# High and low values side by side as 128 weight columns: two products instead of three in the attention of a dilated gMLP decoder

## The chip, the core and the metric

The kernel runs on one NeuronCore of a Trainium2 chip. The time is the device time of one execution in microseconds; the median of three runs is compared. TensorE multiplies (PE in the profile, its weight loads are PEld), VectorE (DVE), ScalarE (ACT) and GpSimd (POOL) do the elementwise work, and SyncE (SP) starts the transfers.

## What is computed

One step of a decoder with two layers. Each layer projects 1024 prompt positions and 64 sample positions (8 streams of 8), mixes them in two branches, a gated gMLP and an attention, and adds the result to the residual stream. The part that matters here is the attention of the prompt: three groups with dilations 1, 4 and 16, eight heads of 64 dimensions each, in which a query reads its own and at most 128 earlier keys of its residue class.

```python
def dilated_band_attention(q, k, v, dil, n_back):
    ...
    s = jnp.einsum('brnqhd,brnkhd->brnhqk', qb, kb,
                   preferred_element_type=jnp.float32) * (HEAD_DIM ** -0.5)
    ...
    s = jnp.where(valid[None, None, :, None], s, NEG)
    lse = jax.nn.logsumexp(s, axis=-1)
    p = jnp.exp(s - lse[..., None])
    o = jnp.einsum('brnhqk,brnkhd->brnqhd', p.astype(vb.dtype), vb,
                   preferred_element_type=jnp.float32)
    ...
    return o, lse

def combine_dilations(outs, lses):
    w = jax.nn.softmax(jnp.stack(lses, axis=0), axis=0)
    return jnp.sum(w[..., None] * jnp.stack(outs, axis=0), axis=0)
```

Everything is fp32.

## The kernel before

**Precision.** The big products run in fp32r, which keeps fewer bits than fp32. Each operand is therefore split into a high part (a rounded copy, by ScalarE) and a low part (the rest, by a subtraction), and a product becomes three: high by high, high by low, low by high. `split` (L242 to L249) makes the parts.

**The stream of jobs.** A layer goes through a list of jobs, each of which multiplies a 128-column slice of the projection weights with the activations of three pieces of 384, 384 and 320 positions (`piece`, L733). A piece is 24 products into a bank `pspj` (L741), three for each of eight key tiles. Between them, behind the 9th, the 18th and the last product, `tick` (L445) lets other work into the instruction streams. Every engine executes its own stream in the order in which it was written, so what stands ahead and waits holds back what stands behind.

**Attention.** A unit is one group and one pair of heads: jobs for values, queries and keys of 128 columns (two heads), 24 units in all, 12 in each layer. A unit has eight blocks of 128 queries, and each block passes three steps, one piece apart. `att_a`: TensorE multiplies queries and keys into `pss` (L870), VectorE adds the mask and takes the extremes (L878), ScalarE takes the exponential (L882). `att_b`: TensorE transposes the probabilities into `pspt` (L895), and ScalarE and VectorE split them into the high and low tile `pt` (every other block uses a spare part of an activation tile, named `act` in the profile). `att_c`, which the change touches: the products of values and probabilities into `pso` (L916), and one ScalarE copy for each head out of `pso` into `oacc` (recorded at L240, in `copy`). A block has one key block or two: always one in the group with dilation 16, alternating in the group with dilation 4, and two but for the first block with dilation 1.

**Values.** `ev_val` (L817) takes a value job out of PSUM. `v_transposes` (L832) transposes four blocks of 128 positions at a time on TensorE (L838) into a `psmi` bank, and `split` writes a tile `vhl` of [128, 2, 512]: 512 high columns, then 512 low ones. A head of a key block is 64 columns in each half.

**Merging.** When the three groups of a head pair are done, `combine` (L958) computes the softmax weights of the groups on a small tile: a chain of eight VectorE operations with one of ScalarE between them (L969 to L977) and a split `ehl`; later it multiplies and adds the three `oacc` tiles (L993 to L999). There are four merges in each layer.

**Buffers.** `pspj` has three banks, `pss` two, and `pspt`, `pso` and `psmi` one each. The next `att_c` can therefore start only when `pso` has been read.

Of the kernel before, what the change touches and what calls it, by code (L numbers as in the profile page):

```python
# [25 lines left out]
FR = mybir.dt.float32r  # L26
AF = mybir.ActivationFunctionType
OP = mybir.AluOpType
# [151 lines left out]
class Builder:  # L180
# [636 lines left out]
    def ev_val(self, l, job, p, ps, st):  # L817
        _, g, pr = job
        if p == 0:
            st["t"] = self.slot([128, T], name="vT")  # L820
        for o, x in self.group_views(st["t"], ps, g, p):
            self.copy(o, x)
        if p == 2:
            t = st["t"]
            self.store(self.a["ov"][l, g, pr], t)
            u = {"l": l, "g": g, "pr": pr, "n": 3 * pr + 2 - g}
            self.cur = u
            u["v"] = [self.slot([128, 2, 512], FR, "vhl") for _ in range(2)]
            for i in range(3):
                self.after(lambda i=i: self.v_transposes(u, t, i), i + 1)  # L830

    def v_transposes(self, u, t, i):  # L832
        nc, ident = self.nc, self.pk("ident")
        if i < 2:
            ps = self.ps("mi")
            for j in range(4):
                b = 4 * i + j
                nc.tensor.transpose(ps[:, j * 128:j * 128 + 128], t[:, b * 128:b * 128 + 128], ident)  # L838
            self.split(u["v"][i][:, 0, :], u["v"][i][:, 1, :], ps)
        else:  # L840
            self.rows_out(t[:, SEQ:T], self.vn_d[u["l"]][u["g"], :, u["pr"] * 128:u["pr"] * 128 + 128])

# [59 lines left out]
    def att_c(self, u, b):  # L902
        nc, g = self.nc, u["g"]
        n = 1 + self.nprev(g, b)
        pt = u["pt"].pop(b)
        ps = self.ps("o")
        for h in range(2):
            first = True
            for j in range(n):
                kb = b - n + 1 + j  # L910
                v = u["v"][kb // 4]
                c = slice((kb % 4) * 128 + 64 * h, (kb % 4) * 128 + 64 * h + 64)
                i = slice(128 * (h * n + j), 128 * (h * n + j) + 128)
                for a, e in ((0, 0), (0, 1), (1, 0)):
                    last = j == n - 1 and a == 1
                    nc.tensor.matmul(ps[0:64, 128 * h:128 * h + 128], v[:, a, c], pt[:, e, i], start=first, stop=last)  # L916
                    first = False
        o = self.oacc[:, u["n"] % 6, :]
        for h in range(2):
            r = slice(64 * h, 64 * h + 64)  # L920
            src = ps[0:64, 128 * h:128 * h + 128]
            if g == 2:
                dst = o[r, 128 * b:128 * b + 128]
            elif g == 1:
                dst = o[r].rearrange("p (m r b i) -> p r b m i", m=4, r=4, b=2, i=32)[:, b // 2, b % 2]
                src = src.rearrange("p (m i) -> p m i", i=32)
            else:
                dst = o[r].rearrange("p (r b i) -> p b r i", r=16, b=8, i=8)[:, b]
                src = src.rearrange("p (r i) -> p r i", i=8)
            self.copy(dst, src)  # L930
        if b == 7:
            for x in ("q", "k", "v"):
                del u[x]
            self.side.append(self.unit_stats(u))
# [770 lines left out]
```

## Time and profile before

| | |
|---|---|
| median of three runs | 3126.67 us (3125.6 to 3132.71) |
| the profiled execution | 3128.81 us |
| its span | 3127.0 us |
| TensorE busy | 3001.5 us, 96%, 19136 products |
| VectorE busy | 1702.8 us, 54% |
| ScalarE busy | 1230.0 us, 39% |
| GpSimd busy | 1363.7 us, 44% |
| mean granted clock of TensorE | 0.983 |

The profile shows one execution. Its page gives the busy time of each engine, the chain of work that ended last, and the costliest groups of instructions; the trace answers questions on a line, a tile or a stretch of time. Durations of products overlap, since TensorE starts the next one before the last has left the array, so what a product costs in a stream is the distance from its start to the next start. In a timeline, instructions of one kind that follow each other stand in one row with their count; the length of that row runs from the first start to the last end.

### The profile page before, as it was taken

The page shows a single profiled execution, that of the slowest core. Times are in us where ns is not written, and L with a number is a line of the kernel's source. Part 1 is how long each engine was busy: PE and PEld are TensorE (multiplying, and loading weights), DVE is VectorE, ACT ScalarE, POOL GpSimd, SP SyncE. Part 2 cuts the span into 40 slices and gives each one's busy share as a digit, 9 for nine tenths or more (in the row PEclk, how much of TensorE's full clock was granted, in tenths as well). Part 3 has the DMA queues.
Part 4 walks back from the last instruction along what each step waited for, and adds up shares of the span by engine and source line. Part 5 has one row for each costly group of instructions (what it writes and reads, how often), then busy time and mean ns, then how long its engine had stood idle before and what let it go on. Part 6 is the DMA issues. An engine that isn't in the chain of part 4 may idle for free.

```text
span 3127.0 us, 51203 instructions
## 1 busy us (share of the span) xinstructions
PE 3001.5 (96%) x19136; PEld 2860.7 (91%) x19136; DVE 1702.8 (54%) x3583; ACT 1230.0 (39%) x3085; POOL 1363.7 (44%) x959
## 2 busy tenths in 40 slices
PE   6998999999999999999999989999999999999998
PEld 4998899989999998879989988999999899999998
DVE  7444545463266656466773555464632757553666
ACT  5454444444233133343434544444442331322433
POOL 4665547463144223123446655564731542322343
PEclk8999999999999999999999999999999999999999
DMA  6335243434354334466544253434344542434665
GB/s 223 117 100 113 97 88 119 94 107 95 111 189 142 105 119 163 162 239 228 194 161 130 91 121 99 88 123 85 119 88 128 176 150 89 137 103 144 220 214 178
DMA packets 251537, 425.93 MB, mean 136 GB/s; under 512 B 103852, under 2 KB 158392, under 8 KB 251288
## 3 DMA queue, kind: packets, MB, share of 16 engines
q1 hardware_dynamic: 251288, 422.65, 44.7%
q8 instruction: 151, 2.47, 0.3%
q14 instruction: 98, 0.80, 0.1%
HBM read 349.96 MB, written 72.61 MB: 135 GB/s over the span
## 4 chain that ended last, share of the span: by engine, by line
PE 82%; DVE 7%; DMA 4%; issue 2%; ACT 2%; POOL 1%; SPq 0%; DVEq 0%; ACTq 0%; POOLq 0%
PE pspj L741 53%; PE pspj L1377 13%; PE pss L870 4%; PE pso L916 3%; PE pspt L895 2%; DMA kq<-in_kc_dram 1%; DMA craw<-in_wada_dram 1%; PE psmi L602 1%; DVE chl L249 1%; PE psmi L993 1%; PE pspt L1310 1%; DVE act L249 1%; PE pspt L1127 1%; PE pso L1127 1%; PE pss L1094 1%
## 5 line engine op out<-in xcount | busy, mean ns | idle before, releaser
L741 PE MATMUL pspj<-act,whi 128*128 128x384 f32 (+1 forms) x7680 | 1965.8, 339 | 6.2 <-DVE act L674 3.7
L741 PEld LDWEIGHTS pspj<-act,whi 128*128 128x128 f32 x7680 | 1350.9, 190 | 42.1 <-issue 6.6
L741 PE MATMUL pspj<-act,wlo 128*128 128x384 f32 (+1 forms) x3840 | 1263.0, 329 | 2.3 <-POOL wlo L247 2.3
L249 POOL TENSOR_TENSOR wlo<-wraw,whi 128x1024 fp32r<-128x1024 f32 x154 | 373.2, 2424 | 906.0 <-ACT whi L243 764.4
L741 PEld LDWEIGHTS pspj<-act,wlo 128*128 128x128 f32 x3840 | 728.2, 190 | 3.4 <-POOL wlo L247 3.4
L1377 PE MATMUL pspj<-act,whi 128*128 128x384 f32 (+1 forms) x1536 | 373.5, 326 | 0.5 <-ACT act L243 0.4
L243 ACT ACTIVATE whi<-wraw 128x1024 fp32r<-128x1024 f32 x280 | 294.0, 1052 | 124.3 <-DMA wraw<-in_wgm_dram 49.4
L247 POOL TENSOR_TENSOR wlo<-wraw,whi 128x512 fp32r<-128x512 f32 x126 | 192.2, 1532 | 325.5 <-ACT whi L243 274.7
L882 ACT ACTIVATE ssb<-ssb,ast 128x128 f32<-128x128 f32 (+1 forms) x384 | 170.2, 444 | 380.4 <-DVE ast L878 380.4
L878 DVE CUSTOM_DVE_ANT_0 ssb<-pss,pack 128x128 f32<-128x128 f32 (+1 forms) x384 | 119.4, 348 | 326.7 <-PE pss L870 325.7
L1377 PEld LDWEIGHTS pspj<-act,whi 128*128 128x128 f32 x1536 | 270.2, 188 | 1.0 <-ACT act L243 0.7
L1377 PE MATMUL pspj<-act,wlo 128*128 128x384 f32 (+1 forms) x768 | 250.3, 326 | 0.3 <-POOL wlo L247 0.3
L1005 ACT ACTIVATE th<-pspj 128x384 f32<-128x384 f32 x168 | 79.2, 471 | 422.3 <-PE pspj L741 375.9
L787 POOL TENSOR_TENSOR r<-r,sin 128x384 f32<-128x384 f32 x144 | 139.1, 966 | 175.7 <-DVE r L786 169.9
L249 DVE TENSOR_TENSOR chl<-craw,chl 128x512 fp32r<-128x512 f32 x182 | 155.4, 882 | 86.8 <-ACT chl L243 85.1
L377 POOL TENSOR_TENSOR kq<-kq,qb 128x1024 f32<-128x1024 f32 x64 | 152.6, 2390 | 66.5 <-DMA kq<-in_kc_dram 32.0
L381 POOL TENSOR_TENSOR kq<-kq,qb 128x512 f32<-128x512 f32 x128 | 167.3, 1312 | 30.3 <-DMA kq<-in_kc_dram 25.3
L386 DVE TENSOR_REDUCE sc<-kq 128x16 f32<-128x1024 f32 x128 | 155.7, 1217 | 13.0 <-POOL kq L377 12.9
L870 PE MATMUL pss<-kz,q 128*128 128x256 f32 x560 | 156.2, 387 | 5.6 <-ACT kz L240 5.6
L430 POOL TENSOR_TENSOR vq<-vq,pv 128x1024 f32<-128x1024 f32 x64 | 134.8, 2115 | 49.2 <-DMA vq<-in_vc_dram 25.9
L1377 PEld LDWEIGHTS pspj<-act,wlo 128*128 128x128 f32 x768 | 144.2, 188 | 0.6 <-POOL wlo L247 0.6
L247 DVE TENSOR_TENSOR wlo<-wraw,whi 128x512 fp32r<-128x512 f32 x126 | 108.0, 858 | 43.7 <-ACT whi L243 40.7
(211 smaller groups left out, 3676.6 us busy)
## 6 DMA issues: line engine op xcount, KB each, us to landing
wraw<-in_win_dram SPq DMA_DIRECT2D x160, 512.0 KB
kq<-in_kc_dram SPq DMA_DIRECT2D x64, 512.0 KB
vq<-in_vc_dram SPq DMA_DIRECT2D x64, 512.0 KB
craw<-in_wada_dram SPq DMA_DIRECT2D x48, 512.0 KB
wraw<-in_wgm_dram SPq DMA_DIRECT2D x48, 512.0 KB
wraw<-in_wo_dram SPq DMA_DIRECT2D x48, 512.0 KB
kq<-in_kc_dram SPq DMA_DIRECT2D x64, 256.0 KB
craw<-in_vc_dram SPq DMA_DIRECT2D x32, 512.0 KB
```

The costliest lines, as they stand in the source:

```text
L243: self.nc.scalar.activation(hi, src, AF.Copy)
L247: e.tensor_tensor(lo[:, c], src[:, c], hi[:, c].bitcast(FT), op=OP.subtract)
L249: (eng or self.nc.vector).tensor_tensor(lo, src, hi.bitcast(FT), op=OP.subtract)
L377: nc.gpsimd.tensor_tensor(v, v, x, op=OP.mult)
L381: nc.gpsimd.tensor_tensor(v[:, f], v[:, 1], x[f], op=OP.mult)
L386: nc.vector.tensor_reduce(sc[:, :, i].rearrange("p h j -> p j h"), ts.pop(i)[0].rearrange("p a (j h d) -> p (a j) h d", h=2, d=64), axis=A ...
L430: nc.gpsimd.tensor_tensor(v, v, p.unsqueeze(3).to_broadcast([128, 2, 8, 64]), op=OP.mult)
L741: nc.tensor.matmul(ps[:, :w], a[:, k, :], h[:, b, k, :w], start=(n == 0), stop=(n == 23))
L787: nc.gpsimd.tensor_tensor(t2, t2, self.sin[:, s], op=OP.mult)
L870: nc.tensor.matmul(s[:, 256 * j:256 * j + 256], u["q"][:, 128 * b:128 * b + 128], self.kz[:, (b - n + j) % 4].rearrange("p h c -> p (h c)" ...
L882: nc.scalar.activation(x[:, h, :w], x[:, h, :w], AF.Exp, bias=st[:, h * 8 + b:h * 8 + b + 1], scale=-1.0, accum_out=st[:, 16 + h * 8 + b:1 ...
L1377: self.nc.tensor.matmul(ps[:, :w], ws[a][:, k, :], hs[b][k][:, :w], start=(n == 0), stop=(n == 3 * nk - 1))
```

## The change

The tile of split values becomes [128, 4, 2, 128]: for each of four key blocks and each of two heads 128 columns, 64 high ones beside 64 low ones. For the first head the high values are the first 64 columns, for the second head the last 64. ScalarE and VectorE write them through access patterns with runs of 64 columns.

In `att_c` a product then has 128 weight columns, high and low, and there are two of them for a head and a key block, with the high and with the low probabilities. All 128 rows of `pso` are written: one half holds the sums of the high values, the other those of the low ones. The product of low values and low probabilities, left out before, is now in the sum.

On the way out, ScalarE copies the half with the low values to `oacc`, and a new VectorE instruction adds the half with the high values to it. Nothing else changes.

```diff
--- before.py
+++ after.py
@@ -825,7 +825,7 @@
             self.store(self.a["ov"][l, g, pr], t)
             u = {"l": l, "g": g, "pr": pr, "n": 3 * pr + 2 - g}
             self.cur = u
-            u["v"] = [self.slot([128, 2, 512], FR, "vhl") for _ in range(2)]
+            u["v"] = [self.slot([128, 4, 2, 128], FR, "vhl") for _ in range(2)]
             for i in range(3):
                 self.after(lambda i=i: self.v_transposes(u, t, i), i + 1)
 
@@ -836,7 +836,11 @@
             for j in range(4):
                 b = 4 * i + j
                 nc.tensor.transpose(ps[:, j * 128:j * 128 + 128], t[:, b * 128:b * 128 + 128], ident)
-            self.split(u["v"][i][:, 0, :], u["v"][i][:, 1, :], ps)
+            v = u["v"][i]
+            pst = list(v.ap[0])[0]
+            hi, lo = [bass.AP(tensor=v.tensor, offset=v.offset + o, ap=[[pst, 128], [256, 4], [w, 2], [1, 64]])
+                      for o, w in ((0, 192), (64, 64))]
+            self.split(hi, lo, ps.rearrange("p (b h d) -> p b h d", b=4, h=2))
         else:
             self.rows_out(t[:, SEQ:T], self.vn_d[u["l"]][u["g"], :, u["pr"] * 128:u["pr"] * 128 + 128])
 
@@ -908,17 +912,15 @@
             first = True
             for j in range(n):
                 kb = b - n + 1 + j
-                v = u["v"][kb // 4]
-                c = slice((kb % 4) * 128 + 64 * h, (kb % 4) * 128 + 64 * h + 64)
+                v = u["v"][kb // 4][:, kb % 4, h, :]
                 i = slice(128 * (h * n + j), 128 * (h * n + j) + 128)
-                for a, e in ((0, 0), (0, 1), (1, 0)):
-                    last = j == n - 1 and a == 1
-                    nc.tensor.matmul(ps[0:64, 128 * h:128 * h + 128], v[:, a, c], pt[:, e, i], start=first, stop=last)
+                for e in range(2):
+                    nc.tensor.matmul(ps[:, 128 * h:128 * h + 128], v, pt[:, e, i], start=first, stop=j == n - 1 and e == 1)
                     first = False
         o = self.oacc[:, u["n"] % 6, :]
         for h in range(2):
             r = slice(64 * h, 64 * h + 64)
-            src = ps[0:64, 128 * h:128 * h + 128]
+            src = ps[:, 128 * h:128 * h + 128]
             if g == 2:
                 dst = o[r, 128 * b:128 * b + 128]
             elif g == 1:
@@ -927,7 +929,8 @@
             else:
                 dst = o[r].rearrange("p (r b i) -> p b r i", r=16, b=8, i=8)[:, b]
                 src = src.rearrange("p (r i) -> p r i", i=8)
-            self.copy(dst, src)
+            self.copy(dst, src[64 - 64 * h:128 - 64 * h])
+            nc.vector.tensor_tensor(dst, dst, src[r], op=OP.add)
         if b == 7:
             for x in ("q", "k", "v"):
                 del u[x]
```

The order of the instructions, on TensorE, at the first block of all (`pso_1193` is its bank, `vhl_880` its values; L838 transposes values, L741 are products of the projection, and the line numbers behind the change are shifted); rows with - stand in the kernel before, with + in the changed one:

```order
 L741 MATMUL pspj_1142<-act_163,wlo_989 128x384
 L838 MATMUL psmi_1179<-pack,vT_1004 128x128 x4
-L916 MATMUL pso_1193<-pt_1108,vhl_880 64x128 x6
+L918 MATMUL pso_1193<-pt_1108,vhl_880 128x128 x4
 L741 MATMUL pspj_1202<-act_164,whi_988 128x320 x2
 L741 MATMUL pspj_1202<-act_164,wlo_989 128x320
```

Six products of 64 output rows have become four of 128; a block with two key blocks goes from twelve to eight. All else on TensorE stands where it stood.

On VectorE, at the end of the first merging, the kernel before (L977 and the split `ehl` are its last steps, L878 the masks of the next block, L249 the split of probabilities, L785 and L786 the rope of a job):

```order
L977 TENSOR_TENSOR ce_3033<-ce_3033,cmx_3032 16x384
L249 TENSOR_TENSOR ehl_3043<-ce_3033,ehl_3043 16x384
L878 ISA ssb_3067,ast_2579<-pss_3065,pack 128x128
L878 ISA ast_2579 128x1
L878 ISA ssb_3067,ast_2579<-pss_3065,pack 128x128
L878 ISA ast_2579 128x1
L249 TENSOR_TENSOR pt_3084<-pspt_3081,pt_3084 128x256
L785 TENSOR_TENSOR r_3101<-pspj_3055,cos_538 128x384
L786 STREAM_SHUFFLE r_3102<-pspj_3055 128x384
```

And the changed kernel at the same place, where L980, L882 and L933 are the merging, the masks and the new additions:

```order
L980 TENSOR_TENSOR ce_3011<-ce_3011,cmx_3010 16x384
L249 TENSOR_TENSOR ehl_3021<-ce_3011,ehl_3021 16x384
L933 TENSOR_TENSOR oacc_542<-oacc_542,pso_3024 64x128 x2
L882 ISA ssb_3045,ast_2565<-pss_3043,pack 128x128
L882 ISA ast_2565 128x1
L882 ISA ssb_3045,ast_2565<-pss_3043,pack 128x128
L882 ISA ast_2565 128x1
L249 TENSOR_TENSOR pt_3062<-pspt_3059,pt_3062 128x256
L785 TENSOR_TENSOR r_3079<-pspj_3033,cos_538 128x384
L786 STREAM_SHUFFLE r_3080<-pspj_3033 128x384
```

Two additions, one for each head, stand between the split `ehl` and the masks of the next block, and two more behind the rope instructions; so it is at each of the 192 blocks. ScalarE's and GpSimd's streams keep their instructions and their order.

## Rows read from the trace of the kernel before

**Rows 1.** The page: busy time of each engine; below, shares of the chain that ended last.

```profile
PE 3001.5 (96%) x19136; PEld 2860.7 (91%) x19136; DVE 1702.8 (54%) x3583; ACT 1230.0 (39%) x3085; POOL 1363.7 (44%) x959
...
PE 82%; DVE 7%; DMA 4%; issue 2%; ACT 2%; POOL 1%; SPq 0%; DVEq 0%; ACTq 0%; POOLq 0%
```

**Rows 2.** Busy us by engine (instructions) in the two attention stretches; then PEclk, DMA, GB/s.

```profile
100.00:700.00 600.00, 575.84 (x3842) 552.40 (x3840) 299.65 (x778) 271.00 (x833) 355.91 (x281) 0.98 0.41 107
1640.00:2330.00 690.00, 667.19 (x4495) 642.69 (x4494) 341.45 (x870) 313.33 (x947) 395.66 (x312) 0.98 0.41 105
```

**Rows 3.** Line 916: duration ns min/median/max, first and last start, form.

```profile
L916 PEld LDWEIGHTS pso<-act,vhl x960: 133/135/230, 129.5 to 2324.6; 128*64 128x64 f32 x192
L916 PE MATMUL pso<-act,vhl x960: 218/223/455, 129.5 to 2324.6; 128*64 128x128 f32 x192
...
L916 PE MATMUL pso<-pt,vhl x720: 218/223/304, 124.8 to 2320.3; 128*64 128x128 f32 x180
```

**Rows 4.** Timeline, PE: start us, length us, line, out<-in, count; a group of twelve.

```profile
602.05 0.88 PE L916 MATMUL pso<-act,vhl 128*64 128x128 f32 x12
602.77 0.56 PE L741 MATMUL pspj<-act,whi 128*128 128x384 f32 x2
```

**Rows 5.** Timeline, PE: a group of six and the stream behind it.

```profile
501.00 0.53 PE L916 MATMUL pso<-act,vhl 128*64 128x128 f32 x6
501.36 0.56 PE L741 MATMUL pspj<-act,whi 128*128 128x384 f32 x2
501.76 0.33 PE L741 MATMUL pspj<-act,wlo 128*128 128x384 f32 x1
501.94 0.51 PE L741 MATMUL pspj<-act,whi 128*128 128x384 f32 x2
502.28 0.33 PE L741 MATMUL pspj<-act,wlo 128*128 128x384 f32 x1
```

**Rows 6.** The page, costliest groups: busy us, mean ns of one, idle before.

```profile
L741 PEld LDWEIGHTS pspj<-act,whi 128*128 128x128 f32 x7680 | 1350.9, 190 | 42.1 <-issue 6.6
```

**Rows 7.** Timeline, PEld: the weight loads of line 579.

```profile
1356.04 0.96 PEld L579 LDWEIGHTS psmi<-pack,arow 18*128 18x128 f32 x8 [1.20 <-ACT arow L240]
```

**Rows 8.** Line 579: duration of one weight load.

```profile
L579 PEld LDWEIGHTS psmi<-pack,arow x96: 181/187/333, 20.0 to 1363.5; 18*128 18x128 f32 x96
```

**Rows 9.** Timeline, PE: four transposes.

```profile
510.81 0.60 PE L895 MATMUL pspt<-pack,ssb 128*128 128x128 f32 x4
```

**Rows 10.** Groups by shape: busy us, mean ns of one, idle before.

```profile
L895 PE MATMUL pspt<-pack,ssb 128*128 128x128 f32 x560 | 94.5, 276 | 21.3 <-DVE act L249 21.3
...
L878 DVE CUSTOM_DVE_ANT_0 ssb<-pss,pack 128x128 f32<-128x128 f32 x208 | 51.8, 286 | 175.9 <-PE pss L870 175.1
```

**Rows 11.** What writes or reads tile pso: duration ns min/median/max.

```profile
L240 ACT ACTIVATE oacc<-pso x384: 249/269/273, 125.6 to 2325.2; 64x128 f32<-64x128 f32 x192
...
L1130 DVE SCALAR_TENSOR_TENSOR sp<-pso,ng,bs x64: 339/343/345, 1062.0 to 2661.6; 128x128 f32<-128x128 f32 x64
...
L1327 DVE TENSOR_TENSOR zbs<-pso,zbs x16: 175/182/183, 917.5 to 2780.2; 64x32 f32<-64x32 f32 x16
```

**Rows 12.** Timeline, all engines, at the end of a merging.

```profile
298.53 0.53 ACT L240 ACTIVATE oacc<-pso 64x128 f32<-64x128 f32 x2
...
298.65 0.55 DVE L249 TENSOR_TENSOR ehl<-ce,ehl 16x384 fp32r<-16x384 f32 x1 [0.67 <-ACT ehl L243]
...
299.11 0.90 PE L916 MATMUL pso<-act,vhl 128*64 128x128 f32 x6 [4.41 <-ACT oacc L240]
299.13 0.27 DVE L878 CUSTOM_DVE_ANT_0 ssb<-pss,pack 128x128 f32<-128x128 f32 x1
```

**Rows 13.** Waits of PE from 100 to 700 us: total us, times, longest.

```profile
PE pspt L895 <- DVE act L249: 11.1, 3, 5.1
PE pso L916 <- ACT oacc L240: 4.4, 1, 4.4
```

## Prediction

> **What bounds the kernel now.** I read the busy table and the chain of waits first [rows 1]: TensorE is busy for 96% of the span and 82% of the chain that ended last lies on it, VectorE has 7% of that chain. Then I asked for the busy times of the two stretches, one in each layer, in which the prompt's attention runs [rows 2]: TensorE 575.84 of 600 us and 667.19 of 690 us, VectorE half busy (299.65 of 600, 341.45 of 690). So in the stage that the change touches TensorE issues nearly without a break, and what counts is how long its instruction stream is. It stands still for 24.2 us in the first stretch and 22.8 us in the second (length less busy time); the largest waits of the first stretch are few and long [rows 13]: the transposes of the probabilities (L895) wait for VectorE's split L249 three times for 11.1 us together, and L916 waits once for 4.4 us for ScalarE's copy out of `pso`.
>
> The next view is line 916 itself, the products that the change rewrites [rows 3]: 960 + 720 = 1680 products, each with its own weight load of 64 columns, although two neighbours use the same weights. 1680 is 104 blocks with one key block (6 products each) and 88 with two (12 each): 24 units of 8 blocks, of which the order of the keys gives 13 and 11 in every three units.
>
> **What a product costs in the stream.** The recorded duration of a product (223 ns) overlaps that of the next, so the price is the distance between starts. In a group of twelve [rows 4] the first starts at 602.05 and the next projection product at 602.77: 0.72 us, 60 ns each. In a group of six [rows 5]: 501.00 to 501.36, again 60 ns. A moving operand of 128 columns and a weight load of 64 columns both fit into 60 ns, and this row alone does not say which of them sets it.
>
> Other rows do. Line 579 multiplies 128-column weights with a moving operand of only 10 columns. Eight of its weight loads in a row span 0.96 us [rows 7], and one lasts 0.187 us [rows 8], so they start (0.96 - 0.187)/7 = 110 ns apart. Ten moving columns can't need that; the load of 128 weight columns does. Four transposes with 128-column loads and 128 moving columns span 0.60 us [rows 9], one 0.276 us [rows 10]: (0.60 - 0.276)/3 = 108 ns. These are plain fp32. That fp32r weights cost the same is seen at the end of each group of L916: the projection product that follows has 128 fp32r weight columns, and its load can hide only behind one short product. In [rows 5] the two products after the group then take 501.76 - 501.36 = 0.40 us, where two of them take 502.28 - 501.94 = 0.34 us in the steady stream behind. So that load needed 60 + 55 or so = 115 ns. The recorded durations agree: 190 ns for the projection's 128-column load [rows 6], 135 ns for the 64-column load [rows 3], 55 ns more.
>
> **The change part by part.**
> *Products.* Each head and key block goes from three products to two, so 560 of 1680 fall away and 1120 stay. Each now loads 128 columns, since high and low values lie side by side. With a load of 112 ns (the middle of 108 to 115) that the product before it can't cover, a block with one key block costs 4 x 112 = 448 ns, the last of these being the seam to the projection, against 6 x 60 + 55 = 415 ns: 33 ns more. A block with two costs 8 x 112 = 896 against 12 x 60 + 55 = 775 ns: 121 ns more. Sum: 104 x 0.033 + 88 x 0.121 = 3.4 + 10.6 = **14 us longer**. With 108 ns it is 104 x 0.017 + 88 x 0.089 = 9.6 us, with 115 ns 4.7 + 12.8 = 17.5 us. Nothing hides it: TensorE has no gaps between those groups [rows 2]. The saving in multiplications is real, but the array waits for weights, and there are 1120 x 128 columns to load now, where 1680 x 64 were loaded.
>
> [...]
>
> *Copy and add.* ScalarE's copy out of `pso` stays: 384 of 64x128 at 269 ns [rows 11]. New are 384 additions on VectorE, one behind each copy, reading `pso` and `oacc`. No row has this form. The bounds are 0.18 us (L1327, 64x32 out of PSUM) and 0.34 us (L1130, 128x128 out of PSUM) [rows 11]; I take 0.29, of L878, which reads 128 columns of PSUM beside SBUF [rows 10]. That is 384 x 0.29 = 111 us of VectorE's time, some 55 us in each attention stretch, which lifts it from 50% to 59% there. The cover is VectorE's idle half. An addition stands behind the two rope instructions of its piece (L785, L786) or behind other work, and waits for ScalarE's copy; queued behind it are the next block's masks (L878), the cache scores (L386) and the split of the probabilities (L249). TensorE asks for `pso` again one piece later, so an addition that ends half a microsecond after the copy delays nobody there.
>
> The cover is gone where VectorE is the late engine: at the merging of the three groups (L969 to L977 and the split behind them), three times in each attention stretch. In [rows 12] the split of the combining weights runs to 299.20; ScalarE's two copies are done at 299.06, and at 299.11 the waiting products of L916 start. With the change, two additions stand behind that split in VectorE's queue: 299.20 + 2 x 0.29 = 299.78 before `pso` is free, and the masks that started at 299.13 start there as well: 0.65 us later. One such pair at each of six places is 4 us; none would be 0, two pairs would be 8. I take **4 us**.
>
> *Layout.* The 48 splits of the values write in runs of 64 columns instead of 512; the same number of elements and instructions, so 0, with TensorE's transposes of other blocks as cover; if strided writes cost ScalarE or VectorE a tenth, it is a few us off the path.
>
> **Sum.** The profiled execution took 3128.81 us (span 3127.0). 3128.8 + 14 + 4 = 3146.8 us. The median of the runs shown is 3126.67, 2.1 us less than that execution; for a median I predict **3145 us**, 0.6% more. Its own range runs from 9.6 + 0 to 17.5 + 8: 3136 to 3152.
>
> **The rivals.**
> *B, the wide load is no dearer (faster).* If the load of 128 fp32r columns ran at the pace of 64, each product would stay at 60 ns: 1120 x 60 = 67.2 us instead of 100.8, 33.6 us less, and with the 4 us of VectorE the median would be 3126.7 - 33.6 + 4 = 3097. For it speaks only that no row has an fp32r load of 128 columns directly before a product of 128 moving columns. It decides from a distance of 90 ns downward (1120 x 90 = 100.8). [...] Chance 7%.
>
> *C, no change.* The load is partly covered, at some 86 ns: 1120 x 86 = 96.3, 4.5 us gained, which the 4 us of VectorE take back: 3126 us. [...] Against it: every row with 128 columns. Or the low end of the main case with a lucky turn at the stalls (9.6 us longer, some of it falling into TensorE's waits): 3133. Chance 14%.
>
> *D, VectorE becomes late (much slower).* The added instructions wait for ScalarE in VectorE's queue. If in one block of ten the pair of additions and the pair of copies before it (2 x 0.29 + 2 x 0.27 = 1.1 us) end up on the path, 192 x 0.1 x 1.1 = 21 us come on top of the 14: 3126.7 + 35 = 3162. For it: TensorE's long waits in this stage already are waits for VectorE [rows 13], `pso` and `pspt` have one buffer each, and after each merging VectorE has to catch up with less spare time. Against it: half of VectorE's time is free. Chance 17%.
>
> **How the numbers follow.** Main case 62%, B 7%, C 14%, D 17%. The predicted time is the main case, 3145. A measurement can tell about 0.3%, 9.4 us, from no change: slower is over 3136, faster under 3117. So slower 0.79, same 0.14, faster 0.07. The range leaves out B, the lower end of C and the upper part of D: 3126 to 3165.
>
> **What would show it.** In the changed kernel's trace the groups of four products should start 110 ns apart, a group of eight taking about 0.9 us to the next steady projection product; the recorded weight load should be near 190 ns. The additions should appear 384 times with 0.2 to 0.35 us, VectorE near 59% in the two stretches, and the waits for `pso` should name VectorE's addition, six times and half a microsecond longer. The forecast is wrong if the products stay at 60 ns apart (B), or if TensorE's waits in the two stretches grow by over 15 us (D).

## The result and the profile after

The changed kernel takes 3155.95 us (median of four executions, 3153.37 to 3158.45) against 3127.5 us: ratio **1.0072, interval 1.0052 to 1.0091**. A second comparison on another occasion gave 3157.32 against 3130.43, ratio 1.0091 (1.0076 to 1.0105). By these ratios it is slower by 22 to 28 us. The kernel before was run many more times beside the experiments; over 49 of its executions the median is 3130.9, so the first three runs shown ahead were on the low side.

The page of the changed kernel, busy table and shares of the chain, answering [rows 1]:

```profile
PE 3028.3 (96%) x18576; PEld 2889.2 (92%) x18576; DVE 1806.1 (57%) x3967; ACT 1237.3 (39%) x3085; POOL 1364.4 (43%) x959
...
PE 82%; DVE 8%; DMA 4%; issue 2%; ACT 2%; POOL 1%; SPq 0%; DVEq 0%; ACTq 0%; POOLq 0%
```

There are 560 products fewer (18576 for 19136), and TensorE is busy 27 us longer. Line 916 has become L918; its durations, by operand, answer [rows 3]:

```profile
L918 PEld LDWEIGHTS pso<-act,vhl x640: 186/192/338, 131.1 to 2348.0; 128*128 128x128 f32 x160
L918 PE MATMUL pso<-act,vhl x640: 221/274/446, 131.1 to 2348.1; 128*128 128x128 f32 x160
...
L918 PE MATMUL pso<-pt,vhl x480: 221/274/328, 126.4 to 2343.7; 128*128 128x128 f32 x160
```

A weight load is recorded with 192 ns where it was 135. What counts is the distance of the starts; the timeline of TensorE at a group of eight and at a group of four, both behind a projection product, to be held against [rows 4] and [rows 5]:

```profile
2342.95 1.00 PE L918 MATMUL pso<-pt,vhl 128*128 128x128 f32 x8
2343.79 0.51 PE L741 MATMUL pspj<-act,whi 128*128 128x320 f32 x2
2344.14 0.31 PE L741 MATMUL pspj<-act,wlo 128*128 128x320 f32 x1
...
528.87 0.56 PE L918 MATMUL pso<-pt,vhl 128*128 128x128 f32 x4
529.27 0.57 PE L741 MATMUL pspj<-act,whi 128*128 128x384 f32 x2
529.67 0.34 PE L741 MATMUL pspj<-act,wlo 128*128 128x384 f32 x1
```

Four products take 529.27 - 528.87 = 0.40 us, and the seam behind them takes 0.40 us for two projection products, as before. The first load of the group starts with the projection product before it, at 528.70 and so 0.17 us ahead of its own product; the first distance is 60 ns, and each further one is 111: 60 + 3 x 111 = 393 ns. Eight take 2343.79 - 2342.95 = 0.84 us, 60 + 7 x 111 = 837 ns. Taken over all groups at the full clock that stand between projection products (56 and 60 of them, medians), a group with its seam costs 449 ns where six products cost 417, and 896 where twelve cost 769. That is 32 and 127 ns more, 104 x 0.032 + 88 x 0.127 = **14.5 us**. This gives the groups that stand elsewhere the same price. Set one by one beside their counterparts of the kernel before (180 of the 192, at the full clock and without a wait near them), the groups come to 15.8 us: the 14 groups of four that stand behind L996 cost 93 ns more each instead of 32.

The busy times of the attention's stretches, answering [rows 2] (the stretch now ends 10 and 25 us later):

```profile
100.00:710.00 610.00, 586.44 (x3623) 564.19 (x3622) 345.61 (x950) 274.50 (x835) 357.95 (x283) 0.97 0.40 106
...
1655.00:2355.00 700.00, 676.09 (x4205) 652.54 (x4204) 387.03 (x1053) 314.79 (x943) 396.06 (x311) 0.98 0.42 104
```

VectorE went from 50% to 57% and 55%. TensorE stands still for 23.6 us in the first and 23.9 us in the second, against 24.2 and 22.8 before: its waits hardly grew. So the weight loads explain 14.5 us, TensorE's waits there some half a microsecond, and 7 to 13 us are left.

The two traces say where they are. The changed span is 29.7 us longer. The stretches in which TensorE's granted clock stands at half took 12.2 us more from it (66.7 us against 54.5, half the length of these stretches), and over the whole span TensorE stands still 2.9 us longer (128.4 us against 125.5, length less busy time). The remaining 14.6 us fit the price of the loads.

### The profile page after: what moved, and what is told of

Read it like the earlier page. It is cut to its first block, busy times and chain, and to the rows that moved or that the text cites. A ratio compares the mean times of both kernels' runs of the same rounds, so it can differ in the third digit from the quotient of the medians.

```text
span 3156.7 us, 50519 instructions
## 1 busy us (share of the span) xinstructions
PE 3028.3 (96%) x18576; PEld 2889.2 (92%) x18576; DVE 1806.1 (57%) x3967; ACT 1237.3 (39%) x3085; POOL 1364.4 (43%) x959
## 4 chain that ended last, share of the span: by engine, by line
PE 82%; DVE 8%; DMA 4%; issue 2%; ACT 2%; POOL 1%; SPq 0%; DVEq 0%; ACTq 0%; POOLq 0%
PE pspj L741 53%; PE pspj L1380 13%; PE pso L918 4%; PE pss L874 4%; PE pspt L899 2%; PE psmi L602 1%; DVE chl L249 1%; DMA craw<-in_wada_dram 1%; PE psmi L996 1%; DMA wraw<-in_watt_dram 1%; PE pspt L1313 1%; DVE vq L415 1%; DMA kq<-in_kc_dram 1%; PE pspt L1130 1%; PE pso L1130 1%
## 5 line engine op out<-in xcount | busy, mean ns | idle before, releaser
L741 PE MATMUL pspj<-act,whi 128*128 128x384 f32 (+1 forms) x7680 | 1970.7, 340 | 6.4 <-DVE act L674 3.5
L741 PEld LDWEIGHTS pspj<-act,whi 128*128 128x128 f32 x7680 | 1356.3, 191 | 42.1 <-issue 6.6
L741 PE MATMUL pspj<-act,wlo 128*128 128x384 f32 (+1 forms) x3840 | 1266.5, 330 | 2.2 <-POOL wlo L247 2.2
L249 POOL TENSOR_TENSOR wlo<-wraw,whi 128x1024 fp32r<-128x1024 f32 x154 | 373.6, 2426 | 928.1 <-ACT whi L243 814.9
L741 PEld LDWEIGHTS pspj<-act,wlo 128*128 128x128 f32 x3840 | 730.2, 190 | 3.4 <-POOL wlo L247 3.4
L882 DVE CUSTOM_DVE_ANT_0 ssb<-pss,pack 128x128 f32<-128x128 f32 (+1 forms) x384 | 119.6, 349 | 184.1 <-PE pss L874 182.5
L249 DVE TENSOR_TENSOR chl<-craw,chl 128x512 fp32r<-128x512 f32 x182 | 154.2, 875 | 91.3 <-ACT chl L243 90.8
L240 ACT ACTIVATE oacc<-pso 64x128 f32<-64x128 f32 x384 | 104.2, 271 | 216.3 <-DVE oacc L933 149.6
L933 DVE TENSOR_TENSOR oacc<-oacc,pso 64x128 f32<-64x128 f32 x384 | 108.3, 282 | 123.3 <-ACT oacc L240 121.5
L430 POOL TENSOR_TENSOR vq<-vq,pv 128x1024 f32<-128x1024 f32 x64 | 135.1, 2121 | 47.3 <-DMA vq<-in_vc_dram 22.8
```

The costliest lines, as they stand in the source:

```text
L249: (eng or self.nc.vector).tensor_tensor(lo, src, hi.bitcast(FT), op=OP.subtract)
L430: nc.gpsimd.tensor_tensor(v, v, p.unsqueeze(3).to_broadcast([128, 2, 8, 64]), op=OP.mult)
L741: nc.tensor.matmul(ps[:, :w], a[:, k, :], h[:, b, k, :w], start=(n == 0), stop=(n == 23))
```

## Experiments

In the table, the mean clock is the mean granted TensorE clock over the span, averaged over the executions. It stands at two levels in the traces of both kernels, 1.00 and 0.50 of the full clock, so a mean of 0.98 says that 4% of the span ran at half. In the changed kernel three projection products of 384 columns take 0.96 us where it stands at 0.50 (968.49 to 969.45 us) and 0.52 us where it stands at 1.00 (972.18 to 972.70 us). So span times mean clock is, as an estimate, roughly the time that the same stream would take at the full clock throughout; it separates a longer stream from a slower clock. The clock is known to three digits, so one execution's product is good to 1.6 us.

| kernel | executions | median us | ratio to before (interval) | mean clock | span x clock |
|---|---|---|---|---|---|
| before | 49 | 3130.9 | | 0.9815 | 3071.5 |
| changed, first | 4 | 3155.95 | 1.0072 (1.0052 to 1.0091) | 0.978 | 3086 |
| changed, again | 5 | 3157.32 | 1.0091 (1.0076 to 1.0105) | 0.978 | 3087 |
| wide products, no addition | 4 | 3145.75 | 1.0043 (1.0028 to 1.0058) | 0.9815 | 3085.5 |
| before with an addition | 10 | 3135.47 | 1.0010 (0.9998 to 1.0022) | 0.981 | 3073 |
| two narrow products | 4 | 3100.79 | 0.9905 (0.9886 to 0.9923) | 0.981 | 3041 |
| copies first | 4 | 3150.58 | 1.0067 (1.0044 to 1.0089) | 0.979 | 3084 |
| 96 columns | 1 | 3122.79 | | 0.981 | 3062 |
| before, 1.1 us later | 10 | 3134.18 | 1.0010 (0.9995 to 1.0025) | 0.980 | 3073 |
| before, 2.2 us later | 10 | 3138.97 | 1.0025 (1.0012 to 1.0038) | 0.980 | 3075 |
| changed, 2.3 us later | 4 | 3151.66 | 1.0058 (1.0036 to 1.0080) | 0.981 | 3090 |

**Wide products without the addition**

```diff
             self.copy(dst, src[64 - 64 * h:128 - 64 * h])
-            nc.vector.tensor_tensor(dst, dst, src[r], op=OP.add)
```

> The changed kernel without the VectorE addition: two products with 128 weight columns, then ScalarE's copy of the low half alone (the high half is left out of the output). Theory: the price of the change is the weight loads, 14.5 us over 192 blocks (groups of four 32 ns, groups of eight 127 ns longer than six and twelve), and the additions cost next to nothing, so this kernel stays 14 us or more over the kernel before: 3142 to 3156, the upper end if the stretches with half the clock that the changed kernel shows come with it. Rival, the additions are the price: then the time falls back to 3127 to 3140.

Measured: 3145.75, ratio 1.0043, which is 13.5 us over the kernel before on the same chip, at the same mean clock. Span times clock is 14 us up and does not differ from that of the full change. The wide products alone make the whole of the longer stream. Yet this kernel is 10 us below the changed one: the additions are not in the stream's length, but with them the mean clock is 0.978 instead of 0.9815.

**The kernel before with an addition**

```diff
             self.copy(dst, src)
+            nc.vector.tensor_tensor(dst, dst, src, op=OP.max)
```

> The kernel before with a VectorE instruction of the added kind behind each ScalarE copy (maximum of oacc and pso, which leaves the value as it is), products as before. Theory: 108 us of VectorE work in the gaps, at most the six places at the mergings, 0 to 5 us: 3127 to 3133. Rival, the additions and the alternation of ScalarE and VectorE are half of the 28 us: 3138 to 3145.

Measured: ratio 1.0010, interval from nothing to 0.22%, so 0 to 7 us, with 3 us the best value. The absolute time, 3135.47, is over what the theory gave, but the kernel before itself stood at 3132.0 there. The instruction reads and writes what the changed kernel's does and takes nearly as long (277 ns in the mean, 282 there); the group of lines by shape in this kernel:

```profile
L931 DVE TENSOR_TENSOR oacc<-oacc,pso 64x128 f32<-64x128 f32 x384 | 106.3, 277 | 114.0 <-ACT oacc L240 112.5 <-issue 0.3
```

VectorE spends 106.3 us on it and waits 112.5 us for ScalarE, and at equal clock the kernel gets some 2 us longer. All the rest is hidden.

**Two narrow products**

```diff
-                for a, e in ((0, 0), (0, 1), (1, 0)):
-                    last = j == n - 1 and a == 1
+                for a, e in ((0, 0), (0, 1)):
+                    last = j == n - 1 and e == 1
```

> The kernel before with two products of 64 weight columns instead of three (high values by high and by low probabilities; low values by high probabilities are left out). Theory: a product with 64 columns stays at 60 ns and 560 of them are gone, 33.6 us less: 3090 to 3098. Rival, the number of weight columns isn't what sets the distance (a product costs the same whatever it loads): the change's own count, 560 fewer, would then have saved as much, and this kernel would stand where the changed one does, over 3140.

Measured: 3100.79, ratio 0.9905, 30 us less; the time lies 3 us above the range expected. This kernel and the one with wide products alone have the same number of products and no addition; they differ in the columns of their weights, 64 and 128, and by 45 us at equal clock. A group of eight on its TensorE:

```profile
517.90 0.64 PE L916 MATMUL pso<-act,vhl 128*64 128x128 f32 x8
518.38 0.51 PE L741 MATMUL pspj<-act,whi 128*128 128x320 f32 x2
```

0.48 us, 60 ns each as in [rows 4]. Of the 33.6 us expected, some 3 did not show in the time. They are not in the attention's waits: from its first product into `pso` to its last, the attention is 18.2 us shorter in the first layer and 15.2 us in the second in this trace, 33.4 us together, and TensorE stands still there for 43.3 us against 45.9 before. Where they are stays open; the comparison is good to some 3 us.

**96 columns**

The layout is changed too: the high values are the first 64 columns for both heads, so that the 96 columns are all of the high values and half of the low ones. The main lines of the edit are:

```diff
-              v = u["v"][kb // 4][:, kb % 4, h, :]
+              v = u["v"][kb // 4][:, kb % 4, h, 0:96]
...
-                    nc.tensor.matmul(ps[:, 128 * h:128 * h + 128], v, ...
+                    nc.tensor.matmul(ps[0:96, 128 * h:128 * h + 128], v, ...
...
-            self.copy(dst, src[64 - 64 * h:128 - 64 * h])
-            nc.vector.tensor_tensor(dst, dst, src[r], op=OP.add)
+            self.copy(dst, src[0:64])
```

> The changed kernel with 96 weight columns instead of 128: the high values and half of the low ones (the other half is left out, and only the high rows are copied out, without an addition). Theory: the load sets the distance, 0.8 to 0.9 ns for each column, so products start 85 to 88 ns apart, and 1120 of them take about what 1680 at 60 ns took: within 8 us of the kernel before at the same clock. Rival, a load is cheap up to 64 columns and costs 111 ns above: 111 ns apart and 14 us over it.

Its group of eight:

```profile
526.53 0.82 PE L918 MATMUL pso<-act,vhl 128*96 128x128 f32 x8
527.18 0.51 PE L741 MATMUL pspj<-act,whi 128*128 128x320 f32 x2
```

0.65 us: a first distance of 60 ns, as in the groups above, and seven of 85. One execution at the clock 0.981 gave 3122.79, 8 us below the kernel before on that chip and some 10 below it at equal clock, a little better than the 8 allowed for. The groups' medians, 313 and 653 ns against 360 and 719 before, make 104 x 0.047 + 88 x 0.066 = 10.7 us; the first distance of each group, 60 ns instead of 85, is the reason. Loads of 64, 96 and 128 columns go with 60, 85 and 111 ns. From 64 to 96 and from 96 to 128 the distance grows by 25 and 26 ns; there is no step above 64. So above 64 columns the load sets the distance; whether it does at 64 too, or the 128 moving columns do, these runs do not tell.

**Copies first**

```diff
             self.copy(dst, src[64 - 64 * h:128 - 64 * h])
-            nc.vector.tensor_tensor(dst, dst, src[r], op=OP.add)
+            adds.append((dst, src[r]))
+        for dst, src in adds:
+            nc.vector.tensor_tensor(dst, dst, src, op=OP.add)
```

The reason for this run is in the changed kernel's trace at the end of the first merging, answering [rows 12]:

```profile
298.85 0.27 ACT L240 ACTIVATE oacc<-pso 64x128 f32<-64x128 f32 x1
...
298.86 0.55 DVE L249 TENSOR_TENSOR ehl<-ce,ehl 16x384 fp32r<-16x384 f32 x1 [0.65 <-ACT ehl L243]
299.33 0.27 DVE L933 TENSOR_TENSOR oacc<-oacc,pso 64x128 f32<-64x128 f32 x1
299.63 0.27 ACT L240 ACTIVATE oacc<-pso 64x128 f32<-64x128 f32 x1 [0.51 <-DVE oacc L933]
299.94 0.29 DVE L933 TENSOR_TENSOR oacc<-oacc,pso 64x128 f32<-64x128 f32 x1 [0.33 <-ACT oacc L240]
300.26 0.29 DVE L882 CUSTOM_DVE_ANT_0 ssb<-pss,pack 128x128 f32<-128x128 f32 x1
...
300.37 0.45 PE L918 MATMUL pso<-act,vhl 128*128 128x128 f32 x1 [8.54 <-DVE oacc L933]
```

The second copy waits for the first addition, and both write the same tile `oacc`: the four steps run one after another, 298.85 to 300.23.

> The changed kernel with ScalarE's two copies ahead of the two additions, instead of copy, addition, copy, addition. In the changed kernel's trace the second copy waits for the first addition 190 times, 149.6 us together. Theory: those waits are off the path except at the six mergings, some 0.3 to 0.5 us each, 2 to 3 us less: 3150 to 3157. Rival, the alternation is on the path: 10 us or more less, 3146 or below.

Measured: 3150.58, ratio 1.0067, which does not differ from the changed kernel's; 1 to 2 us less at equal clock, which is within the scatter. In its trace TensorE waits 8.6 us at this merging, as in the changed kernel (8.5). The alternation is off the path, as the theory had it.

**The same kernels again, for the clock**

The rest is in the clock: 0.978 instead of 0.9815 of some 3155 us, some 10 us. By the first two traces 10.2 us of it fall outside the prompt's attention, in the sample attention, into which the change does not reach. Its two long waits are the same in both kernels. Waits of TensorE from 890 to 960 us before, and from 900 to 972 us after (total us, times, longest):

```profile
PE pspt L1299 <- DVE qb L1295: 2.0, 1, 2.0
PE pss L1223 <- DVE qb L1213: 1.7, 1, 1.7
```

```profile
PE pspt L1302 <- DVE qb L1298: 2.0, 1, 2.0
PE pss L1226 <- DVE qb L1216: 1.7, 1, 1.7
```

But the granted clock (the number behind the five engines' busy times) is not. Stretches around the two waits, before and after:

```profile
900.00:920.00 20.00, 17.96 (x103) 16.19 (x102) 16.13 (x22) 7.07 (x18) 6.17 (x3) 1.00 0.53 174
920.00:965.00 45.00, 41.73 (x284) 38.93 (x283) 36.94 (x48) 15.89 (x48) 24.84 (x11) 1.00 0.41 138
```

```profile
910.00:930.00 20.00, 17.96 (x93) 16.14 (x92) 14.35 (x22) 6.33 (x17) 5.98 (x3) 0.91 0.52 174
930.00:975.00 45.00, 41.74 (x266) 38.94 (x265) 34.54 (x48) 15.94 (x47) 24.40 (x11) 0.92 0.42 138
```

With the same busy time and the same waits, TensorE gets through 93 products instead of 103, and 266 instead of 284: 20 x 0.09 + 45 x 0.08 = 5.4 us lost (5.1 by the clock's own times, half of the 3.4 and the 6.8 us that it stands at 0.50 there), and as much in the second layer.

> The kernel before once more, for the mean granted clock of further executions and a second trace. In the trace shown ahead the sample attention of both layers ran at the full clock, in the changed kernel's trace 5.1 us were lost there in each layer to stretches at half the clock, behind waits that both have. Theory: whether such a wait is followed by a stretch at half the clock differs from execution to execution, so this trace shows some there too, and the time goes with the clock: 3124 to 3138. Rival, the change causes them: this trace has none there.

> The changed kernel once more. Theory: 14.5 us of weight loads, and the rest of the difference follows the mean granted clock of the executions, which varies by 0.002 to 0.004 (6 to 12 us): 3145 to 3158, mean clock between 0.977 and 0.982. Rival, the change lowers the clock for good: no execution over 0.979, median 3155 as before.

Measured: the kernel before again, twelve executions, 3131.76, ratio to itself 1.0004 (0.9991 to 1.0017), mean clock 0.979 to 0.984; its second trace shows the full clock (1.00) around both waits in both layers, so the theory missed here and the rival's line holds. The changed kernel again: 3157.32, no execution over 0.979, again as the rival said, though the theory's wider ranges hold it too; its second trace shows 1.7 us lost there in the first layer and 5.1 in the second. So the lower clock belongs to the changed kernel. What remained open was whether it comes from what the change does, or from when the waits come. The next three runs move the waits without touching the attention.

**The waits moved**

Ahead of the job `ga 0` of each layer, with n = 10 and 20 in the kernel before and 21 in the changed one:

```diff
+                if job == ("ga", 0):
+                    ps = self.ps("mi")
+                    for _ in range(n):
+                        nc.tensor.transpose(ps[:, 0:128], self.pk("ident"), self.pk("ident"))
```

> The kernel before with ten transposes of a constant ahead of the job ga 0 of each layer (1.1 us of TensorE, result unused), so that all that follows, the sample attention with its two long waits among it, comes 1.1 us later. Theory: whether one of these waits is followed by a stretch at half the clock depends on the moment at which it begins, and 1.1 us brings both to the moments they have in the changed kernel's traces: 2.2 us of padding, and some 3.4 to 5.1 us lost in the sample attention of each layer, 3134 to 3146, mean clock 0.978 to 0.980. Rival, the clock falls for what the change does in TensorE or VectorE: no stretch at half the clock there, 2.2 us more than before, mean clock 0.981 to 0.983.

> The same with twenty transposes (2.2 us later). Theory: another moment, at most one of the two waits is followed by a stretch at half the clock: 4.4 us of padding and 0 to 3.4 us in each layer. Rival as in the run with ten: 4.4 us and none.

> The changed kernel with 21 transposes there (2.3 us later), which brings the two waits to the moments that they have in the traces of the kernel before. Theory: the 5.1 us that were lost in the sample attention of a layer go, and 4.6 us of padding come: 3147 to 3156, mean clock up from 0.978 to 0.980 or more. Rival: the clock stays at 0.978 and the time rises by the padding, 3158 to 3162.

The kernel before, 1.1 us later, at the same places in the first and the second layer:

```profile
900.00:920.00 20.00, 18.07 (x93) 16.49 (x94) 14.61 (x22) 5.21 (x11) 5.41 (x3) 0.91 0.50 172
920.00:965.00 45.00, 41.72 (x284) 38.92 (x283) 36.28 (x48) 16.45 (x48) 24.84 (x11) 1.00 0.42 138
2455.00:2475.00 20.00, 17.96 (x93) 16.13 (x92) 14.04 (x21) 6.83 (x18) 6.48 (x3) 0.91 0.51 169
2475.00:2520.00 45.00, 41.73 (x266) 38.92 (x265) 36.25 (x49) 15.96 (x47) 23.84 (x11) 0.92 0.41 138
```

The changed kernel, 2.3 us later:

```profile
910.00:930.00 20.00, 17.96 (x103) 16.29 (x102) 16.00 (x23) 7.07 (x18) 5.67 (x3) 1.00 0.51 166
930.00:975.00 45.00, 41.69 (x285) 38.89 (x284) 37.08 (x49) 15.43 (x47) 24.82 (x11) 1.00 0.39 138
```

Moved by 1.1 us, the kernel before has three of the four stretches at half the clock that the changed one has (the one behind the second wait of the first layer is missing). Moved by 2.3 us, the changed kernel has none there, in either layer, and its mean clock rises to 0.981: its four executions stand at 0.980 and 0.981, the nine unmoved ones at 0.979 or below. Though it does 4.6 us more work, its median is 4 to 6 us lower than unmoved; the intervals of the ratios overlap, so this gain is less sure than the clock's.

So the lower clock there is not tied to the change's own instructions: in either kernel the same waits keep the clock or lose it when 1.1 or 2.3 us of other work stand 180 us ahead of them. That it goes by the moment at which the waits begin is the reading that fits, but that moment is not the time from the start of the span. The products behind the first wait (first start) in the kernel before, the same 1.1 us later, the changed kernel, and the same 2.3 us later:

```profile
L1299 PE MATMUL pspt<-qb x32: 383/430/500, 902.7 to 2765.1; 24*128 24x512 f32 x16, 24*64 24x512 f32 x16
L1299 PE MATMUL pspt<-qb x32: 383/428/500, 901.9 to 2771.6; 24*128 24x512 f32 x16, 24*64 24x512 f32 x16
L1302 PE MATMUL pspt<-qb x32: 383/427/500, 912.5 to 2794.4; 24*128 24x512 f32 x16, 24*64 24x512 f32 x16
L1302 PE MATMUL pspt<-qb x32: 383/429/500, 912.2 to 2788.8; 24*128 24x512 f32 x16, 24*64 24x512 f32 x16
```

In the first layer the padded kernels leave this wait no later than the unpadded ones (and in the kernel before 1.1 us later it lasts 2.6 us, not 2.0), since what lies ahead of it differs from execution to execution as well (the second trace of the kernel before has 900.1 there), and still one of each pair loses the clock and the other does not. What the moment would be counted from instead, no run shows. Why the loss then comes out alike in the executions of one kernel stays open. Two things did not come as expected. The kernel before lost less in the mean of its executions than in its trace (mean clock 0.980 and 3 us over the kernel before, where 3134 to 3146 was expected and 3134.18 measured; by the time alone the rival's 2.2 us fits as well), so not each execution need lose what the trace lost. And at 2.2 us the trace showed stretches at half the clock behind one wait of the first layer and both of the second (mean clock of that execution 0.980), where at most one in each was expected. Which moment is a bad one can't be read from these runs.

In the prompt's attention itself the two traces of the changed kernel lose 1.7 us more to the clock in the first layer and 3.4 in the second. It stands at three of the six merges, the second of the first layer and the first two of the second; stretches of 20 us around them, before and after:

```profile
455.00:475.00 20.00, 14.92 (x96) 14.34 (x94) 16.41 (x36) 8.42 (x28) 12.34 (x12) 0.91 0.32 98
2008.00:2028.00 20.00, 14.91 (x96) 14.30 (x96) 16.64 (x37) 8.46 (x28) 12.33 (x12) 0.91 0.30 94
1840.00:1860.00 20.00, 14.11 (x86) 13.42 (x84) 15.35 (x29) 6.63 (x21) 13.05 (x12) 0.83 0.27 83
```

```profile
455.00:475.00 20.00, 14.93 (x81) 13.97 (x80) 16.53 (x36) 7.08 (x22) 11.65 (x9) 0.83 0.29 90
2021.00:2041.00 20.00, 14.91 (x84) 13.97 (x83) 16.25 (x35) 7.71 (x23) 11.05 (x10) 0.83 0.29 88
1853.00:1873.00 20.00, 11.45 (x57) 10.89 (x56) 15.10 (x33) 6.81 (x23) 12.13 (x13) 0.75 0.24 72
```

In sum the kernel with wide products and no addition does not show that loss, but by place it does in part: at the second merge of either layer it loses 3.4 us like the changed kernel (1.7 before), and the second trace of the kernel before loses 3.4 us at the second merge of the second layer. So this part is not the additions' alone; what decides it was not told apart.

## Why the prediction was right, point by point

- **What bounds it**: right. TensorE's stream in the attention counts, and its waits there stayed at 47 us in all.
- **The price of a product**: right. Expected were 448 and 896 ns for the groups with their seam, measured 449 and 896; the bounds of 9.6 to 17.5 us held the 14.5. The kernel with wide products alone and the one with two narrow products confirm it from both sides, 14 us up and 30 us down. Rival B (60 ns) and rival C (86 ns) fall: the distance is 111 ns. No run shows the 86 ns of rival C for 128 weight columns; the 85 ns that were measured belong to 96.
- **The additions**: their number and duration were right (286 ns median, 108.3 us in all), the term was not. 4 us were put on the path; at equal clock the addition alone costs 2 us, and beside wide products nothing that can be told (in time, leaving them out beside wide products gave back 10 us, through the clock). The step at the merging failed in its count: six places were expected, and in the whole trace TensorE waits for the addition four times, twice for long, at one merging of each layer. At the other mergings it waits for `pspt` as before (5.0 us, 5.1 before). Where it does wait for `pso`, copy and addition take turns from 298.85 to 300.23. That wait, now 8.5 us, takes the place of two: the 4.4 us of [rows 13], and 3.3 us that stood 11 us ahead of it, L870 for ScalarE's `kz`, in the kernel before:

```profile
284.33 1.22 PE L870 MATMUL pss<-kz,q 128*128 128x256 f32 x2 [3.34 <-ACT kz L240]
```

So 0.8 us came on top here, near the 0.65 expected for one place, and over the whole stretch TensorE does not stand still longer (23.6 us against 24.2). Waits of TensorE in the changed kernel from 100 to 710 us:

```profile
PE pspt L899 <- DVE act L249: 10.0, 2, 5.0
PE pso L918 <- DVE oacc L933: 8.9, 2, 8.5
```

- **The layout**: right, nothing. The 48 splits of the values take 597 ns on ScalarE and 691 on VectorE (median), 597 and 692 before.
- **Rival D** falls with the additions' term: VectorE has time to spare. Its additions wait 121.5 us for ScalarE, and ScalarE's second copies 149.6 us for additions, but TensorE waits for them four times only, 18.1 us in all, where it mostly stood still before too.
- **What was missing**: the clock. The sum had no term for it, and it is some 10 us of the difference. It explains why the time, 3155.95, lies over the main case's own range (to 3152) while its main term was right. That the stated range, to 3165, holds it is luck: the upper part was there for rival D, which did not come. With less of that loss, the changed kernel moved by 2.3 us, less its padding, stands at 3151.66 - 4.6 = 3147, 2 us from the forecast.
- **The median**: the three runs shown ahead were 4 us below the median of 49, which the forecast took over.

## What to carry to other kernels

Here a product of 128 moving columns costs what its weight load costs as soon as the weights have 96 or 128 columns (85 and 111 ns), and the load goes by their number: two products with 128 columns cost more (2 x 111 = 222 ns) than three with 64 (3 x 60 = 180 ns). So count columns loaded (1120 x 128 against 1680 x 64 here), not products, before packing two operands side by side. And when a change shifts everything behind it, compare the mean clock of several executions, or span times clock, before giving the difference to the change's own instructions.

## What the hardware showed that was not expected

In these kernels weights are loaded anew for each product, also where two neighbours use the same ones: the changed kernel has 18576 loads for 18576 products. The distance between fp32r products of 128 moving columns is 60, 85 and 111 ns for 64, 96 and 128 weight columns. One and the same wait of 2 us on TensorE was followed by a stretch at half the clock in some traces and not in others (over the 20 us around it in the first layer, 0.91 in the changed kernel's first trace and 1.00 in that of the kernel before); 2.3 us of useless work ahead of it in each layer brought the changed kernel's mean clock from 0.978 to 0.981.
